# A LayerNorm-GELU kernel: buffer 0 loaded as rows 1, 1 and 2, the last buffer stored as rows 2, 1 and 1

## The chip, the cores and the metric

The kernel runs on one core of one Trainium2 chip. Its time is the device time of one execution in microseconds, the median of several. The span in a profile (first to last instruction) is about 2 us shorter. All runs quoted were at a granted clock of 1.00.

## The reference, cut to what matters

```python
x: (8, 1024, 2048) float32;  gamma, beta: (2048,) float32
mean = np.mean(x, axis=-1, keepdims=True)
var = np.var(x, axis=-1, keepdims=True)
out = gamma * (x - mean) / np.sqrt(var + eps) + beta
return 0.5 * out * (1 + np.tanh(np.sqrt(2 / np.pi) * (out + 0.044715 * out ** 3)))
```

67 MB have to be read and 67 MB written.

## The kernel before

The 8192 rows of x are cut into 16 buffers of 128 partitions x 4 rows (4 MB each). Five buffers in SBUF are used in turn, and the result overwrites the input in its buffer. SyncE issues the loads, ScalarE the stores. VectorE (DVE in the profiles) computes statistics and scales by gamma, TensorE adds beta in PSUM, ScalarE normalizes and applies GELU. A load of a buffer waits until the store of five buffers ago has landed.

```python
R = 4; SLOTS = 5
def by_row(b):
    return b == B - 1
...
# SyncE: buffer 0 in four DMAs of one row, with a semaphore each; the others in one DMA
for b in range(B):
    s = slot(b)
    if stored(b):
        sy.wait_ge(s_store[s], stored(b))
    for q in range(R):
        if b == 0:
            sy.dma_start(out=xts[s][:, q:q + 1], in_=xg[0, :, q:q + 1]).then_inc(s_first[q], 16)
    if b:
        sy.dma_start(out=xts[s], in_=xg[b]).then_inc(s_load[s], 16)
...
# ScalarE, after the GELU of row q of buffer b: the last buffer is stored row by row
if by_row(b):
    ins.then_inc(s_r, 1)
    ac.dma_start(out=og[b, :, q:q + 1], in_=xt[:, q:q + 1])._wait_ge(s_r, b + q + 1).then_inc(...)
    ac.sem_inc(s_g, 1)
elif q == R - 1:
    ...  # one DMA for the whole buffer
```

## Time and profile before

| | before |
|---|---|
| median of 3 runs, and their range | 319.69 us, 319.49 to 319.76 |
| span of the profile | 317.8 us |
| busy share DVE / ScalarE / TensorE | 83% / 80% / 77% |
| moved | 134.27 MB in 5571 packets, mean 423 GB/s |

The prediction shows the lines that carry the reading: the DMA share of nearly 1 from 3 to 313 us. Two more groups, from the page's list of costs and its list of DMA issues, fit it. In the first, the number after the second bar is the idle time of DVE ahead of this line, then what ended most of it; in the others the last number is the median time from issue to landing.

```profile
L148 DVE BATCH_NORM_STATS2 sts<-xt 128x6 f32<-128x512 f32 x256 | 163.5, 681 | 23.7 <-DMA xt<-in_x_dram 21.7
xt<-in_x_dram SPq DMA_DIRECT2D x15, 4096.0 KB, 24.3
out_dram<-xt ACTq DMA_DIRECT2D x15, 4096.0 KB, 37.0
```

DVE idles almost only for loads (21.7 of the 23.7 us ahead of this line). At 433 GB/s a 4 MB transfer needs 9.7 us by itself; loads take 24 and stores 37 because they queue. Between them the two queues keep the engines full, and stores are the longer line.

### The profile page before, as it was taken

To read this page: it belongs to the slowest core of one execution; us is meant where nothing else is said; L and a number is where in the kernel's file an instruction comes from. 1 tells how busy PE (TensorE), PEld (TensorE's weight loads), DVE (VectorE), ACT (ScalarE), POOL (GpSimd) and SP (SyncE) were. 2 spreads that over 40 slices of the span, in tenths; PEclk is the share of its full clock that TensorE was granted. 3 is DMA by queue.
4 is the path that set the end of the run, shared out by engine and by line. 5 is a ranking of instruction groups with operands and counts; after the bars stand their busy time and mean duration, and the time that the engine had idled before them with its cause. 6 is when DMAs were issued, how large, how long until landed. Compare 5 with 4: busy or idle time off the path is not lost.

```text
span 317.8 us, 2075 instructions
## 1 busy us (share of the span) xinstructions
PE 244.3 (77%) x520; PEld 57.1 (18%) x520; DVE 265.0 (83%) x514; ACT 253.9 (80%) x132; POOL 79.0 (25%) x73
## 2 busy tenths in 40 slices
PE   2769988888888898888877868598595895868810
PEld 1211222111212122211111111122121111112100
DVE  3499999999999999999969799696996969879500
ACT  2679999999999999999969779696995969968920
POOL 1033323232323231323213222231312213212000
DMA  7999999999999999999999999999999999999994
GB/s 291 438 462 396 459 396 445 412 454 404 458 400 459 422 437 445 412 450 408 458 417 441 437 421 454 404 458 412 450 433 425 450 408 450 408 458 421 437 404 206
DMA packets 5571, 134.27 MB, mean 423 GB/s; under 512 B 656, under 2 KB 704, under 8 KB 704
## 3 DMA queue, kind: packets, MB, share of 16 engines
q1 hardware_dynamic: 2736, 67.11, 49.4%
q10 hardware_dynamic: 2832, 67.13, 49.1%
q14 instruction: 3, 0.02, 0.0%
HBM read 67.13 MB, written 67.11 MB: 422 GB/s over the span
## 4 chain that ended last, share of the span: by engine, by line
DMA 44%; DVE 27%; ACT 19%; PE 3%; issue 2%; ACTq 1%; DVEq 0%; SPq 0%
DMA out_dram<-xt 27%; DVE sts L148 15%; DMA xt<-in_x_dram 15%; ACT yk L201 12%; DVE zg L164 9%; ACT xt L208 7%; PE ps L226 2%; DMA rows<-in_gamma_dram 2%; DVE mvs L157 2%; DVE nms L141 1%; ACTq L216 1%; DVE ves L158 1%; PE ps L243 1%; ACT g_t L197 1%; ACTq L211 0%
## 5 line engine op out<-in xcount | busy, mean ns | idle before, releaser
L148 DVE BATCH_NORM_STATS2 sts<-xt 128x6 f32<-128x512 f32 x256 | 163.5, 681 | 23.7 <-DMA xt<-in_x_dram 21.7
L201 ACT ACTIVATE yk<-xt,nms,rss 128x2048 bf16<-128x2048 f32 x64 | 134.1, 2095 | 41.7 <-DVE nms L141 41.2
L243 PE MATMUL ps<-zg,ident 128*128 128x512 bf16 x256 | 120.8, 627 | 50.9 <-DVE zg L164 50.9
L132 POOL TENSOR_TENSOR rss<-ves,mhalf 128x1 f32<-128x1 f32 x64 | 78.0, 1219 | 216.5 <-DVE ves L158 157.0
L239 PE MATMUL ps<-b_hl,ones_b 33*128 33x512 bf16 x256 | 120.6, 624 | 2.2 <-PEq L234 2.2
L208 ACT ACTIVATE xt<-ps 128x2048 f32<-128x2048 f32 x64 | 118.8, 1857 | 1.5 <-PE ps L243 1.5
L164 DVE TENSOR_TENSOR zg<-yk,g_t 128x2048 bf16<-128x2048 bf16 x64 | 78.0, 1218 | 5.0 <-ACT yk L201 3.0
L243 PEld LDWEIGHTS ps<-zg,ident 128*128 128x128 bf16 x256 | 27.6, 130 | 144.1 <-DVE zg L164 108.7
L239 PEld LDWEIGHTS ps<-b_hl,ones_b 33*128 33x128 bf16 x256 | 27.0, 127 | 92.1 <-issue 88.4
L157 DVE BATCH_NORM_AGGREGATE mvs<-sts 128x2 f32<-128x24 f32 x64 | 16.9, 264 | 2.2
L141 DVE TENSOR_SCALAR nms<-mvs,rss 128x1 f32<-128x1 f32 x64 | 12.6, 196 | 0.0
L226 PE MATMUL ps<-rows,ones 1*128 1x512 f32 x8 | 7.2, 1072 | 6.0 <-DMA rows<-in_gamma_dram 6.0
L158 DVE TENSOR_SCALAR ves<-mvs 128x1 f32<-128x1 f32 x64 | 9.8, 154 | 2.2
L194 ACT ACTIVATE b_hl<-rows 1x2048 bf16<-1x2048 f32 x1 | 1.9, 1909 | 4.9 <-DMA rows<-in_beta_dram 4.9
L226 PEld LDWEIGHTS ps<-rows,ones 1*128 1x128 f32 x8 | 2.5, 323 | 9.2 <-DMA rows<-in_gamma_dram 6.0
L172 DVE TENSOR_TENSOR b_hl<-rows,b_hl 1x2048 bf16<-1x2048 f32 x1 | 2.3, 2281 | 2.1 <-ACT b_hl L195 2.1
L197 ACT ACTIVATE g_t<-ps 128x2048 bf16<-128x2048 f32 x1 | 1.9, 1877 | 2.4 <-PE ps L226 2.4
L190 ACT ACT_TABLE_LOAD x1 | 1.3, 1283 | 0.9 <-SPq L106 0.9
L167 DVE MEMSET b_hl<- 33x1024 uint32 x1 | 0.9, 912 | 1.2 <-SPq L106 1.2
L195 ACT ACTIVATE b_hl<-rows 1x2048 bf16<-1x2048 f32 x1 | 1.9, 1908 | 0.0
L123 POOL MEMSET ones<- 65x128 f32 x1 | 0.2, 202 | 0.5 <-SPq L106 0.5
L127 POOL TENSOR_SCALAR_AFFINE_SELECT ident<-ident 128x128 bf16<-128x128 bf16 x1 | 0.3, 294 | 0.1
(7 smaller groups left out, 0.9 us busy)
## 6 DMA issues: line engine op xcount, KB each, us to landing
xt<-in_x_dram SPq DMA_DIRECT2D x15, 4096.0 KB, 24.3
out_dram<-xt ACTq DMA_DIRECT2D x15, 4096.0 KB, 37.0
xt<-in_x_dram SPq DMA_DIRECT2D x4, 1024.0 KB, 8.1
out_dram<-xt ACTq DMA_DIRECT2D x4, 1024.0 KB, 12.7
rows<-in_beta_dram ACTq DMA_DIRECT2D x2, 8.0 KB, 5.6
rows<-in_gamma_dram ACTq DMA_DIRECT2D x1, 8.0 KB, 5.0
```

The costliest lines, as they stand in the source:

```text
L132: po.tensor_tensor(out=rss[:, c], in0=ves[:, c], in1=mhalf, op=ALU.pow)._wait_ge(s_a, k + 1).then_inc(s_q, 1)
L141: ve.tensor_scalar(out=nms[:, c], in0=mvs[:, q, 0:1], scalar1=rss[:, c], scalar2=-1.0, op0=ALU.mult, op1=ALU.mult)._wait_ge(s_q, count).th ...
L148: ins = ve.bn_stats(out=sts[:, q, j, :], in_=xr[:, j, :])
L157: ve.bn_aggr(out=mvs[:, q], in_=sts[:, q])._wait_ge(s_o, count + 1).then_inc(s_o, 1)
L158: ve.tensor_scalar(out=ves[:, q:q + 1], in0=mvs[:, q, 1:2], scalar1=float(eps), scalar2=1.0, op0=ALU.add, op1=ALU.mult)._wait_ge(s_o, coun ...
L164: ve.tensor_tensor(out=zgs[q % 2], in0=yks[q % 2], in1=g_t, op=ALU.mult)._wait_ge(s_n, count).then_inc(s_z, 1)
L197: ac.activation(out=g_t, in_=pss[0], func=ACT.Identity)._wait_ge(s_tg, 1).then_inc(s_c, 1)
L201: ac.activation(out=yks[t % 2], in_=xts[slot(b)][:, q], func=ACT.Identity, scale=rss[:, q:q + 1], bias=nms[:, q:q + 1])._wait_ge(s_p, t + ...
L208: ins = ac.activation(out=xt[:, q], in_=pss[i % 2], func=ACT.Gelu_apprx_tanh)._wait_ge(s_t, i + 1)
L226: ins = pe.matmul(pss[0][:, cols(j)], lhsT=ones[64:65], rhs=rows[64:65, j * K // nsub:(j + 1) * K // nsub, :d // K], start=True, stop=True)
L239: ins = pe.matmul(ps[:, cols(j)], lhsT=ones_b, rhs=b_hl[:, cols(j)], start=True, stop=False)
L243: ins = pe.matmul(ps[:, cols(j)], lhsT=ident, rhs=zgs[k % 2][:, cols(j)], start=False, stop=True)
```

## The change

Its intent is fewer and larger transfers at both ends of the run: rows 2 and 3 of buffer 0 come in one DMA, and rows 0 and 1 of the last buffer leave in one. Bytes and compute are the same.

```diff
+FIRST = (slice(0, 1), slice(1, 2), slice(2, 4))
...
-    def by_row(b):
-        return b == B - 1
+    def parts(b):
+        return (2, 1, 1) if b == B - 1 else (R,)
...
-                    for q in range(R):
-                        if b == 0:
-                            sy.dma_start(out=xts[s][:, q:q + 1], in_=xg[0, :, q:q + 1]).then_inc(s_first[q], 16)
+                    if b == 0:
+                        for i, p in enumerate(FIRST):
+                            sy.dma_start(out=xts[s][:, p], in_=xg[0, :, p]).then_inc(s_first[i], 16)
...
-                    if by_row(b):
+                    ends = [sum(parts(b)[:k + 1]) for k in range(len(parts(b)))]
+                    if q + 1 in ends:
+                        k = ends.index(q + 1)
+                        p = slice(q + 1 - parts(b)[k], q + 1)
                         ins.then_inc(s_r, 1)
-                        ac.dma_start(out=og[b, :, q:q + 1], in_=xt[:, q:q + 1])...
+                        ac.dma_start(out=og[b, :, p], in_=xt[:, p])...
```

(Cut: the counts of the semaphores, and DVE's wait, which now falls on the first row of each part.)

More of the change, by code (lines that the diff above doesn't have):

```diff
@@ L68, in sem @@
         return tc.alloc_semaphore(name)
-    s_first = [sem(f"first{q}") for q in range(R)]
+    s_first = [sem(f"first{q}") for q in range(len(FIRST))]
     s_load = [sem(f"load{s}") for s in range(SLOTS)]
@@ L98, in cols @@
         return slice(j * FMAX, (j + 1) * FMAX)
-    def by_row(b):
-        return b == B - 1
+    def parts(b):
+        return (2, 1, 1) if b == B - 1 else (R,)
     def stored(b):
-        return sum(16 * (R if by_row(c) else 1) for c in range(b) if slot(c) == slot(b))
+        return sum(16 * len(parts(c)) for c in range(b) if slot(c) == slot(b))
     with tc.tile_critical(no_gpsimd_drain=True):
@@ L168, in _ @@
                 for q in range(R):
-                    step(slot(0), q, (s_first[q], 16), 2 * q, q - 1 if q else None, q, q)
+                    first = [p.start for p in FIRST]
+                    step(slot(0), q, (s_first[first.index(q)], 16) if q in first else None, 2 * q, q - 1 if q else None, q, q)
                     if q == 0:
@@ L208, in _ @@
                     ins = ac.activation(out=xt[:, q], in_=pss[i % 2], func=ACT.Gelu_apprx_tanh)._wait_ge(s_t, i + 1)
-                    if by_row(b):
+                    ends = [sum(parts(b)[:k + 1]) for k in range(len(parts(b)))]
+                    if q + 1 in ends:
+                        k = ends.index(q + 1)
+                        p = slice(q + 1 - parts(b)[k], q + 1)
                         ins.then_inc(s_r, 1)
-                        ac.dma_start(out=og[b, :, q:q + 1], in_=xt[:, q:q + 1])._wait_ge(
-                            s_r, b + q + 1).then_inc(s_store[slot(b)], 16)
-                        ac.sem_inc(s_g, 1)
-                    elif q == R - 1:
-                        ins.then_inc(s_r, 1)
-                        ac.dma_start(out=og[b], in_=xt)._wait_ge(s_r, b + 1).then_inc(s_store[slot(b)], 16)
+                        ac.dma_start(out=og[b, :, p], in_=xt[:, p])._wait_ge(s_r, b + k + 1).then_inc(s_store[slot(b)], 16)
                         ac.sem_inc(s_g, 1)
```

## The prediction

Where a cut is marked, a statement about the hardware that no trace or run of this case shows was taken out. No term of the sum goes with the cuts: it came to 319.69 - 0.09 = 319.6 us and stands whole. Two arguments go: that 433 GB/s leaves no headroom in the rate, which was not shown, and, in the last rival, why a shift at the front should move the end, and that each engine's work is unchanged.

> **What bounds the kernel now.** I read the page first, its busy shares, its slices and its DMA lines:
>
> ```profile
> PE 244.3 (77%) x520; PEld 57.1 (18%) x520; DVE 265.0 (83%) x514; ACT 253.9 (80%) x132; POOL 79.0 (25%) x73
> DMA  7999999999999999999999999999999999999994
> DMA packets 5571, 134.27 MB, mean 423 GB/s; under 512 B 656, under 2 KB 704, under 8 KB 704
> ```
>
> No compute engine is above 83%, and DVE, the highest, is held up by loads: in the view of waits its bn_stats wait for x eight times, 21.7 us in all. The DMA engines are at nine tenths or more in every slice but the first and the last. So the candidate is the transfers, 67.13 MB in and 67.11 MB out. To see whether they pause anywhere I asked for the busy time by stretch; the columns to read are the last two, the mean busy share of the 16 DMA engines and GB/s (a share a little over 1 is packets that overlap at their ends):
>
> ```profile
> 2.00:3.00 1.00, 0.00 (x0) 0.00 (x0) 0.14 (x1) 0.19 (x1) 0.00 (x0) 1.00 0.84 197
> 12.00:36.00 24.00, 17.90 (x39) 3.84 (x38) 21.63 (x42) 18.98 (x10) 6.96 (x5) 1.00 1.03 443
> 50.00:280.00 230.00, 189.94 (x412) 43.83 (x411) 207.01 (x405) 195.97 (x102) 62.68 (x51) 1.00 1.00 433
> 280.00:304.00 24.00, 17.94 (x39) 3.99 (x37) 17.83 (x34) 19.87 (x11) 4.02 (x4) 1.00 0.99 425
> 304.00:313.00 9.00, 0.00 (x0) 0.00 (x0) 0.00 (x0) 1.29 (x1) 0.00 (x0) 1.00 1.00 423
> 313.00:314.00 1.00, 0.00 (x0) 0.00 (x0) 0.00 (x0) 0.00 (x0) 0.00 (x0) 1.00 0.43 180
> 314.00:316.00 2.00, 0.00 (x0) 0.00 (x0) 0.00 (x0) 0.00 (x0) 0.00 (x0) 1.00 0.12 49
> 316.00:317.80 1.80, 0.00 (x0) 0.00 (x0) 0.00 (x0) 0.00 (x0) 0.00 (x0) 1.00 0.00 0
> ```
>
> The share is 0.99 to 1.03 in every long stretch up to 313 us. Packet by packet the records say the same: summed over the 16 engines and divided by 16, only 0.06 us of idleness lies between 3.0 and 313.2 us. After 313 us it is 0.12, which is two engines of sixteen that finish about 2.5 us after the others; then 1.8 us without packets end the span. Hence the sum: about 2 us before packets flow (first issue 0.94, first packet 1.95), 311.5 us of streaming, 2.5 us for the two late engines, 1.8 us of completion and exit, 317.8 in all. **The bound is DMA throughput from end to end.** It can move only through the number of bytes, the rate, an idle gap put into the stream, or the two ends.
>
> Now the place the second half of the change touches. The timeline of ScalarE shows when the row stores of the last buffer are issued:
>
> ```profile
> 288.90 0.34 ACTq L216 DMA_DIRECT2D out_dram<-xt  x1
> ...
> 293.26 0.34 ACTq L211 DMA_DIRECT2D out_dram<-xt  x1
> ...
> 297.61 0.34 ACTq L211 DMA_DIRECT2D out_dram<-xt  x1
> ...
> 301.97 0.34 ACTq L211 DMA_DIRECT2D out_dram<-xt  x1
> 303.41 1.88 ACT L208 ACTIVATE xt<-ps 128x2048 f32<-128x2048 f32 x1 [1.48 <-PE ps L243]
> 305.32 0.34 ACTq L211 DMA_DIRECT2D out_dram<-xt  x1
> ```
>
> Compute is over at 305.3 us and the engines stream for another 8 us: the store queue is behind. Four rows are 4.19 MB; at the 423 to 427 GB/s of the final stretch they take 9.8 us, so the engines reach row 0 only at about 313.3 - 9.8 = 303.5 us, ten microseconds after its issue. The packet records put the first 8 KB store packets at 303.5 as well.
>
> [...]
> - [...] an issue is 0.34 us on ScalarE and about 0.54 us on SyncE for these rows (four in 2.16 us), a 1 MB row 2.4 us.
> - [...] Here packets are 8 and 32 KB: the records show a median 309 ns and 1213 ns, one following another every 306 and about 1210 ns. Four of 8 KB cost 1224, one of 32 KB 1210: about 14 ns for three boundaries, under 5 ns each. [...]
>
> **The change part by part.**
> 1. Load of buffer 0: four DMAs of one row become rows 0, 1, and 2 with 3. SyncE issues one DMA less, 0.54 us, and the load of buffer 1 is queued that much earlier (about 2.6 instead of 3.15 us). Sixteen engines are then still busy with row 0, which needs 2.4 us of streaming from about 2 us on, so the earlier issue fills no gap: 0 us. On the wait: row 2 now counts as landed only when row 3 has landed too. Four MB from 2 us on, at the 423 GB/s of 3 to 12 us plus a slow first microsecond, are in by about 13 us. DVE needs row 2 not before it has finished row 1, and that had itself waited until 15.23 us for the scaled gamma; the timeline has its first bn_stats on row 2 at 19.36 us. The slack is 6 us: 0 us.
> 2. Store of the last buffer: rows 0 and 1 go in one DMA when row 1 is done, instead of row 0 at 293.26 and row 1 at 297.61. ScalarE loses one issue (0.34 us, and with what goes around it the 0.50 us of idleness shown before the next ACTIVATE; DVE's mean gives part of that back, elsewhere it is 0.26). So I expect the stores at about 297.3, 301.6 and 305.0 us. The engines reach them at 303.5, 303.5 + 4.9 = 308.4 and 310.9 us. Margins 6.2, 6.8 and 5.9 us, all positive: no gap, and compute that ends 0.2 to 0.5 us sooner is hidden: 0 us.
> 3. Packets: the load loses 128 data packets and the store 128 (two of 8 KB become one of 16 KB), and each loses 16 four-byte completion packets. That is 16 data boundaries and 2 completions per engine: 16 x 4.7 ns + 2 x 6 ns = 0.09 us, and this does lie on the bound. It is the only term that does.
>
> Sum: 319.69 - 0.09 = 319.6 us.
>
> **The rivals.**
> - *The coarser first store starves the queue.* This is what grouping would do to a kernel bound by ScalarE: nothing to store between 293.3 and 297.6, so up to 4.4 us lost, 321 to 324 us. Against it: 10 us of backlog at row 0's turn. It needs the backlog of buffer 14's store to be gone six microseconds sooner than it is.
> - *The merged load delays the pipeline at the front.* If row 2 were needed at about 10 us (its landing before) the wait would be up to 2.5 us. But even a late first store (36.4 us now) would not show: the loads of the first five buffers, 21 MB, keep the engines full until nearly 50 us. So about 319.6 even then.
> - *Larger packets give a better rate.* Taking the whole difference between 427 and 433 GB/s for the 4.2 MB concerned, 9.82 against 9.69 us, gives at most 0.13 us: 319.55.
> - *The end of the stream moves.* Two engines end 2.5 us late, so the finish hangs on which engines get held up over the run, by single packets: some 32 KB loads took 1.6 to 2.2 us instead of 1.21. [...] If it tips, the end moves by a fraction of a packet up to one, 1.2 us, either way: 318.5 to 320.9. For: the lag is real. Against: three executions lie within 0.27 us, so it repeats well[...].
>
> **Range and chances.** The computed change of 0.09 us is below the spread of the runs before (319.49 to 319.76). I center on 319.6, and let the range take the last rival at half a packet: 319.0 to 320.2. Two per cent would be 6.4 us; no rival reaches it on either side, the largest being the starved queue at 4.4 us. So within 2% at 0.98, and 0.01 each for faster and slower.
>
> **What would show it.** In the changed kernel: 5571 - 256 - 32 = 5283 packets, 624 of them under 512 B; the load of buffer 1 issued near 2.6 us; no wait of DVE for the joined rows, and bn_stats on row 2 still near 19.4 us; store issues near 297.3, 301.6 and 305.0; a DMA share of about 1 in 293:297, 297:301 and 301:305; the last packets at about 316. I am wrong if one of those stretches shows the share dip by more than what the first 12 us gain, if DVE gets a new wait before 36 us that lasts into a DMA gap, or if the two late engines end much sooner or later than 2.5 us after the others.

## The result, and the profile after

The changed kernel took 319.90 us (median of 6 runs, 319.72 to 320.85), the kernel before 319.73 us (6 runs, 319.46 to 319.98). The ratio is 1.0009 with a 95% interval of 0.9995 to 1.0022: the same. Ratios here are the mean time of a kernel's fast runs over that of the kernel before in the same rounds, so not quite the ratio of the medians quoted.

The same stretches of the changed kernel's profile, with the DMA share and GB/s as the last two columns:

```profile
2.00:3.00 1.00, 0.00 (x0) 0.00 (x0) 0.14 (x1) 0.18 (x1) 0.00 (x0) 1.00 0.75 172
12.00:36.00 24.00, 17.91 (x38) 3.84 (x37) 21.52 (x42) 18.96 (x10) 6.95 (x5) 1.00 1.02 439
50.00:280.00 230.00, 189.03 (x410) 43.68 (x408) 207.05 (x405) 195.91 (x102) 62.62 (x51) 1.00 1.00 433
280.00:304.00 24.00, 18.83 (x41) 4.28 (x40) 17.84 (x34) 19.28 (x10) 4.93 (x4) 1.00 1.00 431
304.00:313.00 9.00, 0.11 (x1) 0.00 (x0) 0.00 (x0) 1.88 (x1) 0.00 (x0) 1.00 0.97 411
313.00:314.00 1.00, 0.00 (x0) 0.00 (x0) 0.00 (x0) 0.00 (x0) 0.00 (x0) 1.00 0.66 279
314.00:316.00 2.00, 0.00 (x0) 0.00 (x0) 0.00 (x0) 0.00 (x0) 0.00 (x0) 1.00 0.16 66
316.00:317.80 1.80, 0.00 (x0) 0.00 (x0) 0.00 (x0) 0.00 (x0) 0.00 (x0) 1.00 0.00 0
```

Little has moved: 433 GB/s in the middle, a share of about 1 to the end, then a few late engines, then the exit. The one visible difference is from 313 to 314 us, 0.66 where it was 0.43: four more engines now finish 0.9 to 1.5 us after the first, while the last packet ends at 316.01 us (316.06 before). The share of 0.97 in 304:313 is not a starved queue: from 300 us on the packet records (the trace's list of single DMA packets) hold 1.89 us of idleness per engine in all, lag of the late engines included, against 2.21 us before.

The prediction named three stretches in which a starved queue would show. Their shares are 0.95, 0.93 and 1.00, and were 0.95, 0.91 and 0.98 before:

```profile
293.00:297.00 4.00, 3.37 (x9) 0.85 (x8) 3.93 (x9) 3.75 (x3) 0.23 (x1) 1.00 0.95 410
297.00:301.00 4.00, 3.58 (x10) 0.85 (x8) 1.10 (x3) 3.50 (x3) 1.23 (x1) 1.00 0.93 401
301.00:305.00 4.00, 2.48 (x6) 0.43 (x4) 1.16 (x1) 2.52 (x2) 0.00 (x0) 1.00 1.00 430
```

The packet count on the page, and the issues of the stores on ScalarE's timeline (start, duration, what):

```profile
DMA packets 5283, 134.27 MB, mean 423 GB/s; under 512 B 624, under 2 KB 672, under 8 KB 672
298.35 0.34 ACTq L216 DMA_DIRECT2D out_dram<-xt  x1
302.70 0.34 ACTq L216 DMA_DIRECT2D out_dram<-xt  x1
306.06 0.34 ACTq L216 DMA_DIRECT2D out_dram<-xt  x1
```

The packets are the 5283 foreseen. The pair of rows is issued at 298.35, and the packet records have its first packet at 303.55 us: 5.2 us in the queue. The stores come about 0.75 us later than rows 1 to 3 did before, not a little earlier as foreseen. DVE's timeline says why: the last buffer's first bn_stats.

```profile
281.04 0.69 DVE L149 BATCH_NORM_STATS2 sts<-xt 128x6 f32<-128x512 f32 x1 [2.57 <-DMA xt<-in_x_dram]
```

Before, it started at 280.06, 0.98 us sooner. In the packet records the slowest engine finished its part of that load 3.48 us after the first engine here, and 1.55 us after it in the kernel before. From this bn_stats to the last store's issue it is 25.26 us before and 25.02 after, so the saved issue on ScalarE is there, 0.24 us; it is merely smaller than the shift, and neither reaches the end.

### The profile page after: what moved, and what is told of

Read it like the earlier page. It is cut to its first block, busy times and chain, and to the rows that moved or that the text cites. A ratio compares the mean times of both kernels' runs of the same rounds, so it can differ in the third digit from the quotient of the medians.

```text
span 317.8 us, 2072 instructions
## 1 busy us (share of the span) xinstructions
PE 244.4 (77%) x520; PEld 57.3 (18%) x520; DVE 265.1 (83%) x514; ACT 253.8 (80%) x132; POOL 79.9 (25%) x73
## 2 busy tenths in 40 slices
DMA packets 5283, 134.27 MB, mean 423 GB/s; under 512 B 624, under 2 KB 672, under 8 KB 672
## 4 chain that ended last, share of the span: by engine, by line
DMA 44%; DVE 28%; ACT 19%; PE 3%; issue 1%; ACTq 1%; DVEq 0%; SPq 0%
DMA out_dram<-xt 26%; DMA xt<-in_x_dram 17%; DVE sts L149 16%; ACT yk L203 12%; DVE zg L165 9%; ACT xt L210 6%; PE ps L226 2%; DMA rows<-in_gamma_dram 2%; DVE mvs L158 2%; DVE nms L142 1%; ACTq L216 1%; DVE ves L159 1%; PE ps L243 1%; ACT g_t L199 1%; DVEq L180 0%
## 5 line engine op out<-in xcount | busy, mean ns | idle before, releaser
L133 POOL TENSOR_TENSOR rss<-ves,mhalf 128x1 f32<-128x1 f32 x64 | 78.9, 1232 | 217.5 <-DVE ves L159 158.1
## 6 DMA issues: line engine op xcount, KB each, us to landing
out_dram<-xt ACTq DMA_DIRECT2D x15, 4096.0 KB, 35.8
```

Source lines behind the costliest of these rows:

```text
L133: po.tensor_tensor(out=rss[:, c], in0=ves[:, c], in1=mhalf, op=ALU.pow)._wait_ge(s_a, k + 1).then_inc(s_q, 1)
```

## The experiments

Each kernel's change is against the changed kernel unless it says otherwise. Each set had its own runs of the kernel before, with medians of 319.69 to 319.70 us, and every ratio is to these.

### The change again, and each half alone

`again_after` is the changed kernel unaltered.

> The changed kernel again, for a second trace and a tighter ratio. Theory (the transfers bound it end to end, only the packet count lies on the bound): ratio to the kernel before 0.9995 to 1.0005, so about 319.7 us; the engines that finish last should again be some 2.5 us behind the first, as in its first trace. Rival (the regrouping shifts the interleaving and costs something): ratio 1.0005 to 1.002, as the first six runs had it (1.0009), with the last load landing later than in the kernel before.

Measured: 320.26 us (5 runs), ratio 1.0011, interval 0.9995 to 1.0027. In its trace the last load again lands late (first bn_stats at 281.09) and nothing else differs.

`load_only`:

```diff
-        return (2, 1, 1) if b == B - 1 else (R,)
+        return (1, 1, 1, 1) if b == B - 1 else (R,)
```

> Only buffer 0 is loaded as rows 1, 1 and 2; the last buffer is stored by row as before. Theory: 319.65 us, ratio 0.9995 to 1.0005; buffer 1's load issued at about 2.3 us; no new wait on DVE before 36 us. Rival (the load's regrouping is what shifts the late engines): this one carries the whole of any difference, about 0.2 us slower, and its last load lands later by 0.5 to 1 us than in the kernel before.

Measured: 319.74 us, ratio 0.9997 (0.9981 to 1.0012). Its last load lands late too (281.04), at no cost. So the part of the rival that puts a difference down to this half falls; the late landing alone is not what costs time.

`store_only`:

```diff
-FIRST = (slice(0, 1), slice(1, 2), slice(2, 4))
+FIRST = (slice(0, 1), slice(1, 2), slice(2, 3), slice(3, 4))
```

> Only the last buffer is stored as rows 2, 1 and 1; buffer 0 is loaded by row as before. Theory: 319.65 us, ratio 0.9995 to 1.0005; the pair of rows issued about 0.25 us earlier than row 1 was, some 5 us before an engine reaches it. Rival (the later first store opens a gap in the stream): DMA share between 297 and 305 us clearly under 0.9, and up to 4 us slower.

Measured: 319.99 us, ratio 1.0005 (0.9990 to 1.0021). The pair was issued at 298.03 us and its first packet came at 303.57. Its front is that of the kernel before, yet its last load also came later (bn_stats at 280.72). What causes that shift is open: the only traces with this bn_stats near 280.0 are those of the kernel before and of `before_delay6` below, and there is one trace of each kernel. Up to that load `store_only` issues the same transfers as the kernel before, so chance is not excluded.

Taken one by one, neither half can be told from zero; the two sets of the changed kernel both lean 0.1% (about 0.3 us) to the slow side, while 0.09 us to the fast side was computed. Taken together, the runs of these two sets say more. The 16 executions with the pair (the changed kernel twice, and `store_only`) average 320.07 us; the 20 with single rows (the kernel before, and `load_only`) average 319.80. The difference is 0.27 us, with a 95% interval of 0.06 to 0.48. So the half with the store probably costs about 0.3 us, and the half with the load nothing. This grouping was made after the results were seen, and the cause is open: the traces with the pair end their last packet at 315.87 to 316.18 us, those with single rows at 316.06 and 316.36, so they do not show the cost.

### How much room the end has: one DMA for the last buffer, and idle work ahead of it

`whole_store`:

```diff
-        return (2, 1, 1) if b == B - 1 else (R,)
+        return (R,)
```

> Only the last buffer is stored in one DMA; buffer 0 is loaded as rows 1, 1 and 2. Theory: the store is issued at about 305.8 us, its first packet is at 306.8, the early engines run dry at 303.8 to 304.2 and the late ones at 306.3; 4.19 MB at 427 GB/s take 9.8 us, so the last packet ends at about 316.6 instead of 316.2 and the late engines are hardly held up: 320.1 to 320.5 us. Rival (the 1.7 us of the kernel with both ends whole is all from this end): 321.3 us.

Measured: 320.04 us (5 runs), ratio 1.0013 (1.0000 to 1.0026). The stretches of its profile:

```profile
280.00:304.00 24.00, 18.81 (x41) 4.28 (x40) 17.84 (x34) 19.52 (x11) 4.94 (x4) 1.00 0.97 421
304.00:306.00 2.00, 0.00 (x0) 0.00 (x0) 0.00 (x0) 1.64 (x1) 0.00 (x0) 1.00 0.08 33
306.00:308.00 2.00, 0.00 (x0) 0.00 (x0) 0.00 (x0) 0.00 (x0) 0.00 (x0) 1.00 1.23 524
308.00:313.00 5.00, 0.00 (x0) 0.00 (x0) 0.00 (x0) 0.00 (x0) 0.00 (x0) 1.00 0.97 419
313.00:316.00 3.00, 0.00 (x0) 0.00 (x0) 0.00 (x0) 0.00 (x0) 0.00 (x0) 1.00 0.81 350
```

This is the instructive trace. Now the queue does run dry: the share is 0.08 from 304 to 306 us, because the only store is issued at 305.67 and its first packet follows 0.84 us later. Yet the last packet ends at 316.42, 0.41 us after the changed kernel's 316.01, and from 300 us to the last packet the idleness per engine is 2.49 us in all, where it was 1.89. The gap of over 2 us falls on the engines that are early and that would otherwise have waited at the end for the late ones. In this trace all sixteen engines finish the last store within 0.17 us of each other. An average DMA share of 0.08 sounded like 2 us lost, and it was under half a microsecond, since the latest engine sets the end.

`after_delay2` and `after_delay6` put idle work ahead of the last buffer's GELU, with m in range(2) and in range(6):

```diff
+    idle = sb("idle", [P, 6, d], mybir.dt.uint8)
...
                     xt = xts[slot(b)]
+                    for m in range(2 if i == T - R else 0):
+                        ac.activation(out=idle[:, m], in_=g_t, func=ACT.Identity)
```

> The changed kernel with two idle ACTIVATEs (about 2.1 us each, into a scratch tile) on ScalarE ahead of the last buffer's first GELU: its stores are issued 4.2 us later. Theory (the end is backlog, with some 4 to 5 us of slack at each of the three stores): issues near 302.5, 306.9 and 310.3 us, first packets 1 us after each, the engines reach them at 303.8, 308.7 and 311.1, so only the early engines stall by a few tenths: 319.7 to 320.4 us. Rival (the late store sets the end): 324 us.

Measured: 319.98 us (4 runs), ratio 1.0013 (0.9996 to 1.0029). The two took 3.69 us and the stores moved to 301.70, 306.05 and 309.41, with no resolvable effect. In its trace the engines come to the pair at 303.57 us, as in `store_only`. So the compute that ends the kernel has more than 3 us of room.

> The same with six idle ACTIVATEs, 12.6 us, so that the engines have run dry before the pair is stored: the backlog is gone. Theory: the end is the last row's issue, 306.1 + 12.6 = 318.7, plus 1.0 to the first packet and 2.45 of transfer, 322.1 instead of 316.3: about 325.7 us.

Measured: 323.47 us (4 runs), ratio 1.0124 (1.0097 to 1.0150). I had taken 2.1 us for an idle ACTIVATE; it took 1.8 (10.89 us for six), which is 1.7 of the 2.2 us by which 325.7 was too high. With the issues as they came the account holds:

```profile
292.61 10.89 ACT L212 ACTIVATE idle<-g_t 128x2048 uint8<-128x2048 bf16 x6
309.03 0.34 ACTq L219 DMA_DIRECT2D out_dram<-xt  x1
313.39 0.34 ACTq L219 DMA_DIRECT2D out_dram<-xt  x1
316.74 0.34 ACTq L219 DMA_DIRECT2D out_dram<-xt  x1
```

The last issue at 316.74, 0.84 us to a first packet (as in `whole_store`) and 2.45 us for a row (1.05 MB at 427 GB/s, an estimate from the rate of the final stretch) make 320.03; the last packet ended at 320.26.

`before_delay6` is the kernel before with the same six.

> The kernel before with the same six idle ACTIVATEs. Theory: the last row is again what ends it, issued at about 305.3 to 306.3 + 12.6 us, so 325.0 to 325.9 us, the same as the changed kernel with this delay within 0.7 us, since a pair of rows is transferred (4.9 us) before the last row is even issued (7.7 us after the pair). Rival (the one in the prediction: without a backlog the pair's late issue costs what row 0 would have moved in the meantime, up to 4.4 us): the changed kernel with this delay is 2 to 4.4 us slower than this one.

Measured: 323.23 us (4 runs, 323.12 to 323.37), ratio 1.0110 (1.0094 to 1.0127). Between the two kernels with this delay there are 0.24 us, although from 306 to 311 us the DMA share is 0.26 with the pair (first line) and 0.67 with single rows (second line):

```profile
306.00:311.00 5.00, 3.64 (x9) 0.85 (x8) 1.35 (x2) 4.50 (x3) 0.00 (x0) 1.00 0.26 111
306.00:311.00 5.00, 3.45 (x9) 0.85 (x8) 1.42 (x3) 4.50 (x4) 0.00 (x0) 1.00 0.67 275
```

In the traces the last row is issued 0.70 us later with the pair (316.74 against 316.04), since the work of the last buffer starts later there too. The prediction's rival had a size of up to 4.4 us for this situation. That size is wrong even on its own premise, that no backlog is left: the engines catch up. From 311 to 316 us the share is 1.00 with the pair and 0.63 with single rows, and after 316 us only 1.6 MB move (2 us at 381 and 4 us at 203 GB/s), less than two rows: the pair has been transferred before the last row is issued at 316.74.

`whole_delay6` is `whole_store` with the same six.

> Buffer 0 loaded as in the changed kernel, the last buffer stored in one DMA, with the same six idle ACTIVATEs. Theory: the one store is issued at 305.7 + 12.6 = 318.3 us and all four rows (9.8 us) follow its first packet at 319.3: the last packet at 329.1, about 332.5 us, 7 us slower than the changed kernel with this delay. That is what splitting the last store is worth where no backlog hides it. Rival (the split is worth nothing even then): within 1 us of the other two.

Measured: 331.09 us (4 runs, two near 330 and two near 332, which is not explained), 7.6 us slower than `after_delay6`. The store was issued at 318.10 and the last packet ended at 328.85. So the split of the last store is worth 7 us, three rows of transfer (7.4 us at 427 GB/s), where compute sets the end; in this kernel, where the queue does, `whole_store` ended its last packet 0.41 us later. What matters in it is that the last part is small; 1, 1, 1, 1 (`before_delay6`, 323.23 us) and 2, 1, 1 (`after_delay6`, 323.47 us) share that.

### The front: one DMA for buffer 0

`whole_load`:

```diff
-FIRST = (slice(0, 1), slice(1, 2), slice(2, 4))
+FIRST = (slice(0, 4),)
```

> Only buffer 0 is loaded in one DMA of four rows; the last buffer is stored as rows 2, 1 and 1. Theory: all work at the end of the span comes about 2 us later (as in the trace with both ends whole), so the last stores are issued at about 300.4, 304.8 and 308.2 us; with 1 us to the first packet that is still before the engines reach them (303.8, 308.7, 311.1), so nothing shows: 319.6 to 320.2 us. Rival (the late start itself costs, since the kernel with both ends whole was 1.7 us slower): 321.3 us.

Measured: 320.49 us (6 runs, 320.17 to 322.05), ratio 1.0036 (1.0020 to 1.0052). This is a miss, 0.3 us above my range, and slower than the kernel before by more than the noise. The stores were issued at 300.15, 304.50 and 307.86 as foreseen, and the engines came to the pair at 304.09, so no gap was opened there. In the one execution with a trace (320.17 us, the fastest) the last packet ended 0.39 us later than in the changed kernel (its repeat: 0.17 us later). The rest of the excess is in executions without a trace and stays open.

`whole_both` has both edits, that of `whole_load` and that of `whole_store`.

> The extreme of the change: buffer 0 loaded in one DMA of four rows and the last buffer stored in one. Theory: at the front DVE waits until about 12.7 us for row 0 and the first store is issued about 2 to 3 us later than 36.4, which the loads of the first five buffers hide until about 50 us: no cost. At the end the one store is issued at about 305 us and needs about 1 us to its first packet; the engines run dry at 303.5 (the late ones at about 306), so a gap of up to 2.5 us opens on the early engines and of about 0.3 us on the late ones, which alone set the end: 319.9 to 320.6 us. Rival (the front matters): over 322 us. Rival (all engines count): about 322 us from the end alone.

Measured: 321.37 us (5 runs), ratio 1.0048 (1.0032 to 1.0064). It shows how the ends add up. Loading four rows at once delays the statistics of row 0 until 13.74 us (5.82 before), and the compute stays late to the end: its store is issued at 308.16 us, not at 305.67. No backlog is left to hide that: in the trace (of the slowest execution, 322.34 us) every DMA engine is idle from 306 to 309 us. Both my expectations of the store's issue (about 305 us) and of the time were too low.

### The packet term, magnified

`rows_all` makes every load and every store a set of four DMAs of one row, except for the last store:

```diff
-                        sy.dma_start(out=xts[s], in_=xg[b]).then_inc(s_load[s], 16)
+                        for r in range(R):
+                            sy.dma_start(out=xts[s][:, r:r + 1], in_=xg[b, :, r:r + 1]).then_inc(s_load[s], 16)
```

(and so on ScalarE for b < B - 1, with the counts of the semaphores to match.)

> Every buffer is loaded and stored as four DMAs of one row (only the last buffer is stored as 2, 1 and 1), so the same bytes go in 8 KB packets instead of 32 KB. This measures the packet term of the prediction, magnified some 45 times: about 720 more packet boundaries and 90 more completions per engine than in the changed kernel, at 4.7 and 6 ns: 3.4 + 0.5 = 3.9 us, so about 323.6 us (322.8 to 324.5). Rival (packet size does not matter): 319.7. Rival (the issue of the stores on ScalarE, four times 0.34 us and more for each buffer, becomes the bound): DMA share under 0.97 between 50 and 280 us and over 326 us.

Measured: 323.33 us (4 runs, 323.25 to 323.42), ratio 1.0114 (1.0099 to 1.0128). The page and the long stretch:

```profile
DMA packets 18388, 134.28 MB, mean 418 GB/s; under 512 B 2080, under 2 KB 2128, under 8 KB 2128
50.00:280.00 230.00, 186.08 (x400) 42.68 (x400) 203.26 (x401) 192.18 (x101) 61.63 (x51) 1.00 1.01 427
```

The share stays at 1 and the rate falls from 433 to 427 GB/s: the engines are as busy, with more overhead. Against the kernel before there are 18388 - 5571 = 12817 more packets, 801 per engine, for 3.64 us: 4.5 ns each. The change removes 18 per engine, so an estimate of 0.08 us from this figure stands beside the 0.09 predicted.

`rows_loads` splits the loads alone.

> Every load goes as four DMAs of one row (8 KB packets), the stores in 32 KB packets as before. Theory: [...] where both have work stores now get four fifths of the rate: they no longer pile up, loads land later, and the backlog that hides the end is gone. The stores of the last buffer then wait for compute and not for the engines: the last load lands later than 290 us and the end is set by the last row's issue plus about 1 + 2.5 us: 323 to 332 us, far more than the packet term alone (2.0 us, 321.7). Rival (the share of the queues does not follow packet size): 321.7 and a last load at about 281 us.

Measured: 331.62 us (4 runs, 328.68 to 333.53), ratio 1.0364 (1.0316 to 1.0412). The issue list and the stretches:

```profile
out_dram<-xt ACTq DMA_DIRECT2D x15, 4096.0 KB, 16.6
50.00:280.00 230.00, 176.32 (x381) 40.69 (x380) 190.25 (x373) 180.36 (x94) 57.68 (x47) 1.00 1.01 426
280.00:304.00 24.00, 16.46 (x36) 3.85 (x36) 22.15 (x44) 20.23 (x11) 6.38 (x5) 1.00 0.76 323
304.00:306.00 2.00, 2.00 (x5) 0.42 (x4) 1.93 (x5) 2.00 (x2) 0.64 (x1) 1.00 0.00 0
```

The rate in the middle is that of `rows_all`, but a store now lands in 16.6 us (35.8 in the changed kernel), and the last load is complete at 290.75 us by the packet records (280.6 there). The packet records show why: from 210 to 220 us, with both queues running, 97 load packets and 108 store packets start, about one for one, so 0.79 MB of loads against 3.54 MB of stores: 0.82 of the bytes, where four fifths were expected. The loads fall behind, and at the end there is no backlog: DMA is idle (a share of 0.00 from 304 to 306 us) while DVE and ScalarE work off the last two buffers. DVE's waits for loads come to 40.0 us. `rows_all`, with the same small loads but small stores too, has none of this. So in these runs it is the queue of stores at the end that hides the compute of the last buffer, and the balance between the two queues that makes it.

## Why the prediction was right

- **The bound.** It said DMA throughput from end to end. The share and 433 GB/s are unchanged after, and `rows_all`, which adds packets (and their issues) but no bytes, adds time while the share stays at 1.
- **Part 1, the load.** It said 0 us, with an earlier load of buffer 1 and 6 us of slack at row 2. The load of buffer 1 was issued at 2.32 us (2.6 foreseen), the joined rows landed at 13.1 us (13 foreseen), DVE's first bn_stats on row 2 began at 19.38 (19.36 before), and `load_only` measured a ratio of 0.9997.
- **Part 2, the store.** It said 0 us, because the margins were positive. The margins were there: the three stretches show no new gap. The pair waited 5.2 us in the queue, and issuing the stores 3.35 us later still (`after_delay2`) cost nothing that could be resolved. The issue times were off by 1 us, since a shift of the last load's landing was not foreseen; the conclusion did not hang on it. What the part left out is the probable 0.3 us that the pooled runs show for the pair; its cause is open, but it is not a starved queue, which the trace would show.
- **Part 3, packets.** The 0.09 us cannot be seen in the change itself; the magnified measurement gives 0.08 us. (It counts 6 ns for a completion packet. In the records of the kernel before, chained by end and start, the next packet mostly starts 5 to 6 ns after it, while its median duration is 9 ns. And the prediction's 0.06 us of idleness before 313.2 us comes to 0.01 us when packets in flight are counted against sixteen. Neither matters.)
- **The sum** was 319.6 us and 319.9 was measured, inside the range of 319.0 to 320.2. The difference of 0.3 us is of the size of the runs' spread, so the sum by itself is not refuted. Its sign is probably wrong, though: the pooled runs put the change at a small loss. That the time fell inside the range is owed to the missing gap; that it came within 0.3 us of the sum shows nothing about the 0.09.
- **The rivals.** A starved queue did not occur. Its size, up to 4.4 us, was a mistake (an idle gap was counted in full, as if the engines could not catch up), as `before_delay6` beside `after_delay6` shows: 0.24 us. The statement on the front, that a late first store would not show, was right for the change; `whole_load`, at a ratio of 1.0036, warns against it in general, though by what route it loses time is open. The lag of the late engines stayed: the sixteen parts of the last store finish within 2.7 us in both kernels' traces, although four more are 0.9 to 1.5 us late in the changed one. So the end did not tip in the traces; whether it is what costs the pair 0.3 us was not tested.

No version here beats the kernel before; 134.27 MB at 433 GB/s are 310 us of its 317.8 us span, so at that rate little is left to take; that no higher rate is possible was not shown.

## What to carry to other kernels

Before regrouping transfers at the end of a kernel, find out when the DMA engines get to them. Where they came out of a backlog here, issue times 3.35 us later did not show (`after_delay2`, ratio 1.0013, interval 0.9996 to 1.0029); where they did not, the size of the last part was worth 7.6 us (`whole_delay6`, 331.09 us, against `after_delay6`, 323.47). In `whole_store` the average DMA share fell to 0.08 for 2 us, and the last packet came 0.41 us later: the gap cost what it delayed the latest engine, far less than its length. The two queues of `rows_loads`, with packets of 8 and 32 KB, did not share the engines equally (0.79 MB of loads to 3.54 MB of stores in 10 us). That run took 11.9 us more than the kernel before, of which its 6336 more packets are an estimated 1.8 us at the 4.5 ns of `rows_all`.
